# DeltaNet queries, keys and values: 128x128 transposes on TensorE replaced by 32x32 block transposes on VectorE and a trip through DRAM

## The chip, the cores and the metric

The kernel runs on one core of a Trainium2 chip. The metric is the device time of one launch in microseconds (us), lower is better. A core has a matrix engine (TensorE, "PE" in the profile), a vector engine (VectorE, "DVE"), an engine for functions (ScalarE, "ACT"), GpSimd ("POOL") and a queue engine (SyncE, "SP") that issues nearly all transfers of this kernel. SBUF is the on-chip memory of 128 partitions, PSUM the accumulator banks that TensorE writes, DRAM the device memory.

## What is computed

One layer of a hybrid decoder trunk: a normalised input is projected, three groups work on the columns (a gated spatial MLP, eight heads of gated DeltaNet, cross-attention), and one output projection brings them together. The change touches the DeltaNet heads, of 128 columns each:

```python
qkv = causal_conv_silu(jnp.concatenate([d_q, d_k, d_v], axis=-1), conv_w[l])
q, k, v = jnp.split(qkv, 3, axis=-1)
q = l2norm(to_heads(q)) * DN_HEAD_DIM ** -0.5
k = l2norm(to_heads(k))
v = to_heads(v)
...
kb = k * beta[..., None]
a = jnp.where(strict, jnp.einsum('bhnid,bhnjd->bhnij', kb, k) * decay, 0.0)
T = lax.linalg.triangular_solve(a + eye, ...)
attn_intra = jnp.where(tri, jnp.einsum('bhnid,bhnjd->bhnij', q, k) * decay, 0.0)
k_dec = k * jnp.exp(g_last[..., None] - g_cum)[..., None]
...
v_new = val_c - jnp.einsum('bhid,bhde->bhie', kcd_c, state)
o_c = jnp.einsum('bhid,bhde->bhie', qg_c, state) + jnp.einsum('bhij,bhje->bhie', ai_c, v_new)
state = state * jnp.exp(gl_c)[..., None, None] + jnp.einsum('bhid,bhie->bhde', kd_c, v_new)
```

There are 1024 tokens, 2048 model columns, and everything is float32. A norm over a head's 128 columns is needed for every token of q and k.

## The kernel before

**Order of work.** The kernel's body doesn't issue instructions. Each call on `V` (DVE), `S` (ACT), `G` (POOL), `PE` and `Q` (SP) is recorded by `Plan.add` (line 136) with the regions of memory that it reads and writes, and priced by `Plan.price` (line 183): a transpose on PE at its passes, a transfer at its bytes over 350 per ns with 3.8 us of latency, and so on. `Plan.issue` (line 382) lays the operations out several times against these prices, with priorities that come from how late each may be, keeps the layout that ends first, and emits all operations in that order. Each engine then works through its own list strictly in order, and so does SP's queue. The order is fixed when the kernel is built; on the chip only semaphores decide when an instruction may start.

**The matrix work.** The large projections run in stages (`project_stage`, line 1469, over `seven`, line 1290): a 2x2 block scheme in which seven products take the place of eight. Every float32 operand is split in a high and a low part (`split_to`, line 540), and a product is three matmuls (`triple`). The stages that matter here, in order: the projection of heads 0 to 3 (line 1544), that of heads 4 to 7 (line 1559), then the gates `d_z` together with the MLP's `v` (`zv`, line 1657), then the remaining columns, and at the end the output projection, in the order of line 1891.

**The heads.** The tokens are handled in two halves (`hf`) of 512 columns, the heads in pairs. Heads 0 to 3 are called early here, heads 4 to 7 late. For each head and half:

- `conv` (line 947) reads the projected columns, with channels on the partitions and tokens along the row, and makes q, k or v by convolution and SiLU in a tile of 128x512.
- `qk` (line 969) needs k and q with tokens on the partitions: for the sums of squares (`sumsq`, line 965) and for the scaled copy `kd` (`by_token`, line 961). `to_tokens` (line 925) makes them with four PE transposes of 128x128 into one PSUM bank, and ACT reads the bank. Then come the products of k and q with k (the bank again), multiplied by the decays `e` into `gt` and `ai`.
- `front` (line 1182) calls these for two heads, with tiles q, k, kd, ai from `front_sets`: for early heads three sets take turns, for late heads there is one, `own_set`, quarters of the tile `os`. The four tiles are stored to DRAM for later.
- `inverse` (line 1019) inverts diagonal blocks for four pairs and halves at a time on DVE: once for all early heads, once for all late heads.
- `back_of` (line 1565) loads the stored tiles again into one pair of sets (`back_sets`), finishes the inverse (`levels`), makes v (`values`, line 1214: conv, four PE transposes, and `by_token` into the tile `vs`), runs the scan over four steps of 128 tokens and writes the head's output.

In lines 1571 to 1575 the backs of early pairs and the fronts of late pairs alternate. In `heads_out` (line 1159) the output is turned already in the way that the change uses: `turn` (line 936) lets DVE transpose each 32x32 block and stores the tile, `turned_in` (line 941) reads it back with four transfers that put the blocks in their places. The early heads' outputs are read back by `gate` (line 1619), which works on the fresh gate columns in the tiles `obs`, of which there are four.

**Tiles that are shared.** `ring["tn"]` has four tiles, given out in turn. `qk` takes one of them a head for the decay row `vs`, `values` takes one a head for v. Before the backs of late pairs one is taken away (line 1679). `ring["inv"]` gives the split parts in `qk` and the two work tiles of `inverse`. An operation that writes a tile waits for all earlier readers of that part of it.

```python
def to_tokens(*pairs):
    with R.together():
        for src, tp in pairs:
            for tt in range(NT):
                PE.transpose(tp[:, tt * P : (tt + 1) * P], src[:, tt * P : (tt + 1) * P], ident)
    return [tok(tp) for src, tp in pairs]
```

Of the kernel before, what the change touches and what calls it, by code (L numbers as in the profile page):

```python
# [11 lines left out]
AF = mybir.ActivationFunctionType  # L12
# [5 lines left out]
P = 128  # L18
# [4 lines left out]
HT = 512  # L23
# [3 lines left out]
NG, NH, NX = 4, 8, 4  # L27
# [374 lines left out]
def kernel(  # L402
# [29 lines left out]
    V, S, G, PE, Q = R.dve, R.act, R.pool, R.pe, R.sp  # L432
    rank, behind = R.rank, R.behind

    def C(shape, name, dt=F32):
        return sb.tile(list(shape), dt, name=name, tag=name)[:]

    def DT(shape, name, dt=F32):
        return dr.tile(list(shape), dt, name=name, tag=name)[:]
# [41 lines left out]
    def tok(ap):  # L481

        return ap.rearrange("p (t c) -> p t c", c=P)
# [15 lines left out]
    ring = {t: Slots(t, 2, [P, HT]) for t in ("kT", "qT", "vs", "kd", "ai")}  # L499
# [6 lines left out]
    jk = C([P, HT], "jk", mybir.dt.bfloat16)  # L506
# [4 lines left out]
    turn = {"acc": 0, "tp": 0, "dn": 0}  # L511
# [23 lines left out]
    def rsqrt_to(o, a):  # L535
        with rank(1):
            G.tensor_tensor(out=o, in0=a, in1=mhalf[:, : a.shape[1]], op=ALU.pow)


    def split_to(hi, lo, src, eng):  # L540
        S.copy(hi, src)
        eng.tensor_tensor(out=lo, in0=src, in1=hi, op=ALU.subtract)
# [7 lines left out]
    def triple(a, l, r, start, stop, cls=9):  # L550

        mm(a, l[0], r[0], start, False, cls)
        mm(a, l[0], r[1], False, False, cls)
        return mm(a, l[1], r[0], False, stop, cls)
# [181 lines left out]
    for mt in range(2):  # L736
        t = [ring["ai"](F32R) for _ in range(2)]
# [9 lines left out]
    for h in range(NX):  # L747
        t = ring["vs"](F32R).rearrange("p (s m) -> p s m", s=2)
# [60 lines left out]
    def over(bufs):  # L809
        r = Ring("", 0, None)  # L810
        r.bufs = bufs
        return r
# [38 lines left out]
    r3, ww = ([steps[:, i * P : (i + 1) * P] for i in two] for two in ((0, 1), (2, 3)))  # L851
    scs = [C([P, 12, NT, NH], f"sc{hf}") for hf in range(2)]
    gcs, ecs = ([DT([NT, NH, P], f"{n}{hf}") for hf in range(2)] for n in ("gcd", "ecd"))
    e_d = [[DT([P, NT, P], f"ed{hf}_{h}") for h in range(NH)] for hf in range(2)]
    scan_banks, work = dnr.bufs[0:2], over(dnr.bufs[0:2])
    dnab = over(scan_banks)
# [68 lines left out]
# [7 lines that stand above are left out]
    def four(t, order):  # L932

        return t.rearrange(f"p ({order}) -> p t b i", b=4, t=NT)

    def turn(tile, src, dst):

        V.transpose(four(tile, "b t i"), four(src, "t b i"))
        Q.dma_start(dst, tile)

    def turned_in(o, src):

        v = src.rearrange("(a j) (b n) -> b j a n", a=4, b=4)
        for b in range(4):
            Q.dma_start(o[b * 32 : (b + 1) * 32].rearrange("j (a n) -> j a n", a=4), v[b])

    def conv(which, h, hf, o):
        ct = which * NH + h
        xr = ring["xr"]()
        w = [cw[:, k * 24 + ct : k * 24 + ct + 1] for k in range(4)]  # L950
        if hf == 0:
            G.memset(xr[:, 0:3], 0.0)
            Q.dma_start(xr[:, 3:], p_d[which][h][:, 0:HT])
        else:
            Q.dma_start(xr, p_d[which][h][:, HT - 3 :])
        S.activation(o, xr[:, 3:], AF.Copy, scale=w[3])
        for k in range(3):
            V.scalar_tensor_tensor(o, xr[:, k : k + HT], w[k], o, op0=ALU.mult, op1=ALU.add)
        S.activation(o, o, AF.Silu)

    def by_token(o, src, scale):
        for tt in range(NT):
            S.activation(o[:, tt], src[:, tt], AF.Copy, scale=scale[:, tt : tt + 1])

    def sumsq(o, src):
        for tt in range(NT):
            S.activation(jk[:, 0:P], src[:, tt], AF.Square, accum_out=o[:, tt : tt + 1])

    def qk(h, hf, tiles, hs, gt, bank):

        q, k = tiles[:2]
        kd, ai, vs = map(tok, (*tiles[2:4], ring["tn"]()))
        beta, edk = (scs[hf][:, i] for i in (0, 4))
        (kt,) = to_tokens((k, bank))
        sumsq(hs[:, 1], kt)
        V.tensor_scalar(hs[:, 1], hs[:, 1], EPS, None, op0=ALU.add)
        V.reciprocal(hs[:, 3], hs[:, 1])
        V.scalar_tensor_tensor(hs[:, 2], hs[:, 3], -1.0, beta[:, :, h], op0=ALU.mult, op1=ALU.mult)
        V.tensor_tensor(out=hs[:, 3], in0=hs[:, 2], in1=edk[:, :, h], op=ALU.mult)
        by_token(kd, kt, hs[:, 3])  # L980
        e = tok(ring["E"]())
        Q.dma_start(e, e_d[hf][h])
        Q.dma_start(vs, ecs[hf][:, h].partition_broadcast(P))
        by_token(e, e, hs[:, 2])
        (qt,) = to_tokens((q, bank))
        sumsq(hs[:, 0], qt)
        V.tensor_scalar(hs[:, 0], hs[:, 0], P * EPS, P * EPS * EPS, op0=ALU.mult, op1=ALU.add)
        rsqrt_to(hs[:, 4], hs[:, 1])
        V.tensor_tensor(out=hs[:, 4], in0=hs[:, 4], in1=hs[:, 1], op=ALU.mult)

        ch, cl = (ring["inv"](F32R).rearrange("p (t s c) -> p t s c", s=2, c=P) for _ in range(2))
        for i, src in enumerate((k, q)):
            split_to(ch[:, :, i], cl[:, :, i], tok(src), V)
        for t2 in range(NT // 2):
            d = bank
            for j in range(2):
                tt = 2 * t2 + j
                triple(d[:, j * 2 * P : (j + 1) * 2 * P], (ch[:, tt, 0], cl[:, tt, 0]), (ch[:, tt], cl[:, tt]),
                       True, True, R.cls)
            dv = d.rearrange("p (t s c) -> p t s c", s=2, c=P)  # L1000
            ts = slice(2 * t2, 2 * t2 + 2)
            V.tensor_tensor(out=gt[:, ts], in0=dv[:, :, 0], in1=e[:, ts], op=ALU.mult)
            V.tensor_tensor(out=ai[:, ts], in0=dv[:, :, 1], in1=e[:, ts], op=ALU.mult)
        V.tensor_tensor(out=q, in0=q, in1=vs.rearrange("p t c -> p (t c)"), op=ALU.mult)
# [154 lines left out]
    def heads_out(hf, hp, hss, rest):  # L1159
        obs = [vs for kd, ai, vs in rest]  # L1160

        for hs, ob in zip(hss, obs):
            sumsq(hs[:, 5], ob)
            V.scalar_tensor_tensor(hs[:, 6], hs[:, 5], 1.0 / P, hs[:, 0], op0=ALU.mult, op1=ALU.add)
            rsqrt_to(hs[:, 7], hs[:, 6])
            by_token(ob, ob, hs[:, 7])
        for h, (kd, ai, vs) in zip(hp, rest):
            kd, ai, y = (t.rearrange("p t c -> p (t c)") for t in (kd, ai, vs))
            turn(kd, y, o_d[hf][h])
            if h >= NJ:  # L1170
                e = sums()
                Q.dma_start(e, g_d[hf][h - NJ])
                turned_in(ai, o_d[hf][h])
                normed(kd, ai)
                V.tensor_tensor(out=y, in0=kd, in1=e, op=ALU.mult)
                head_done(h, hf, y)
# [5 lines left out]
    def front(p, hf, banks):  # L1182

        hp = (2 * p, 2 * p + 1)
        gt = ring["gt"]().rearrange("p (h t i) -> p h t i", h=2, i=P)
        for i, h in enumerate(hp):
            tiles, hs = front_sets(), ring["hs"]()
            conv(1, h, hf, tiles[1])
            conv(0, h, hf, tiles[0])
            qk(h, hf, tiles, hs, gt[:, i], banks[i])  # L1190
            V.tensor_copy(late_hs[:, hf, h], hs[:, 0:5:4])
            for d, t in zip(late_d[hf][h], tiles[:4]):
                Q.dma_start(d, t)
        gdr = blocks_out(gt, f"{hf}{p}")
        Q.dma_start(gt_d[hf][p].rearrange("p (h t i) -> p h t i", h=2, i=P), gt)
        return gdr
# [16 lines left out]

    def values(hf, hp, gt, qs, ks, hss, rest, inv):
        for i, h in enumerate(hp):
            v = ring["tn"]()
            conv(2, h, hf, v)
            bank = scan_banks[i]
            by_token(rest[i][2], to_tokens((v, bank))[0], hss[i][:, 4])

    def back(hf, hp, gt, qs, ks, hss, rest, inv, ut=None):
        ut = ut or levels(gt, *inv)
# [339 lines left out]
    scan_banks, work = [dnr.bufs[0]] * 2, over(dnr.bufs[0:1])  # L1562
    gdrs = []

    def back_of(p, hf, inv):
        state = front_late(p, hf, inv)
        ut = levels(state[2], *state[-1])
        values(*state)
        back(*state, ut)
# [106 lines left out]
    scan_banks, work = dnr.bufs[0:2], over(dnr.bufs[2:3])  # L1676
# [46 lines left out]
    for n, (tag, to) in enumerate((("gt", mkT), ("inv", mv))):  # L1723
        for i in range(NX // 2):
            t = ring[tag](F32R).rearrange("p (h s m) -> p h s m", h=2, s=2)
# [107 lines left out]
    tn = ring["tn"].bufs  # L1833
# [88 lines left out]
```

## Time and profile before

| | |
|---|---|
| time, median of 3 runs | 1594.69 us (1593.5 to 1596.71) |
| profiled execution: time, span of its instructions | 1593.81 us, 1592.1 us |
| granted TensorE clock, mean | 0.997 |
| instructions | 24568 |
| matmul records on PE (transposes among them) | 8349 |
| bytes moved by transfers | 434.12 MB |

A share is busy time over the span. Busy time of PE counts the union of its records, and since matmuls are pipelined, the record of one (0.39 us for 512 columns) overlaps the next, which starts 0.23 us later; what one occupies is read from the starts. Transposes on PE show as MATMUL with `ident` as one input, block transposes as STREAM_TRANSPOSE on DVE. Nearly all instructions stand under one line, since a plan issues them, so groups are told apart by the names of their tiles: in `out<-in` a name stands without its number, `dn` and `acc` are PSUM banks, `od` is the DRAM tile of the heads' outputs, `sm` the tiles into which `gate` reads it back.

### The profile page before, as it was taken

How to read it: one execution, taken by the hardware profiler on the slowest of the kernel's cores; microseconds unless marked ns; L12 is line 12 of the kernel's file. 1: busy time of each engine (PE TensorE's matmuls, PEld its weight loads, DVE VectorE, ACT ScalarE, POOL GpSimd, SP SyncE). 2: the span in 40 equal slices, each digit the busy share in tenths (PEclk: the TensorE clock that was granted, in tenths of full speed). 3: DMA queues.
4: the chain of work that ended last, by engine and by line, in shares of the span. 5: the costliest groups of instructions: out<-in, count | busy, mean ns of one | idle time of the engine just before them, and what ended most of it. 6: DMA issues, size and time to landing. Idle time of an engine off the chain costs nothing.

```text
span 1592.1 us, 24568 instructions
## 1 busy us (share of the span) xinstructions
PE 1570.2 (99%) x8349; PEld 1315.3 (83%) x8349; DVE 1228.7 (77%) x1818; ACT 963.3 (61%) x2006; POOL 106.7 (7%) x143
## 2 busy tenths in 40 slices
PE   8999999999999999999999989999999999999997
PEld 7988888888887888888888878888888888888886
DVE  6977655877589997777789996867658888688875
ACT  6833255535698436787886557765658864344455
POOL 0100010001000100111111001000000000000001
PEclk9999999999999999999999999999999999999999
DMA  9999966888679898786888988999877989778647
GB/s 320 327 317 346 284 171 183 294 292 245 218 246 315 298 325 254 257 250 205 282 281 277 303 244 245 341 325 309 268 245 253 298 298 347 235 263 293 232 146 276
DMA packets 335951, 434.12 MB, mean 273 GB/s; under 512 B 70089, under 2 KB 160466, under 8 KB 335826
## 3 DMA queue, kind: packets, MB, share of 16 engines
q1 hardware_dynamic: 334098, 429.39, 83.3%
q0 software_dynamic: 1088, 2.10, 0.4%
q8 instruction: 66, 1.08, 0.3%
q10 hardware_dynamic: 640, 1.07, 0.2%
q14 instruction: 59, 0.48, 0.1%
HBM read 332.78 MB, written 99.16 MB: 271 GB/s over the span
## 4 chain that ended last, share of the span: by engine, by line
PE 92%; ACT 3%; DMA 2%; DVE 1%; issue 1%; SPq 0%; POOL 0%; POOLq 0%; ACTq 0%; DVEq 0%
PE acc L398 56%; PE dn L398 35%; ACT jk L398 1%; ACT rhi L398 1%; DMA h0d<-tn 1%; SPq L398 0%; DMA tn<-vd 0%; DMA ut<-in_x_dram 0%; DMA kept<-in_mem_dram 0%; DVE rlo L398 0%; DMA raw<-in_w_in_dram 0%; DVE vs L398 0%; ACT vs L398 0%; DVE tn L398 0%; ACT inv L398 0%
## 5 line engine op out<-in xcount | busy, mean ns | idle before, releaser
L398 PE MATMUL acc<-lh,rhi 128*128 128x512 f32 x1024 | 396.2, 396 | 2.9 <-DVE obs L398 1.2
L398 PE MATMUL acc<-lh,rlo 128*128 128x512 f32 x1024 | 382.9, 397 | 0.0
L398 ACT CAST rhi<-raw 128x1024 fp32r<-128x1024 f32 (+1 forms) x148 | 186.6, 1261 | 248.8 <-PE dn L398 133.8
L398 DVE TENSOR_TENSOR rlo<-raw,rhi 128x1024 fp32r<-128x1024 f32 (+1 forms) x148 | 219.3, 1482 | 109.0 <-ACT rhi L398 98.8
L398 PE MATMUL acc<-ll,rhi 128*128 128x512 f32 x688 | 268.0, 395 | 0.8 <-DVE ll L398 0.8
L398 PEld LDWEIGHTS acc<-lh,rhi 128*128 128x128 f32 x1024 | 192.3, 188 | 41.1 <-issue 1.5
L398 PEld LDWEIGHTS acc<-lh,rlo 128*128 128x128 f32 x1024 | 191.9, 188 | 37.4
L398 DVE TENSOR_TENSOR ll<-ll,lh 128x1024 fp32r<-128x1024 f32 x122 | 148.5, 1217 | 17.3 <-ACT lh L398 17.0
L398 PEld LDWEIGHTS acc<-ll,rhi 128*128 128x128 f32 x688 | 129.6, 189 | 26.4 <-DVE ll L398 1.3
L398 ACT CAST lh<-ll 128x1024 fp32r<-128x1024 f32 x122 | 128.2, 1051 | 29.5 <-PE dn L398 9.0
L398 PE MATMUL acc<-lm,rhi 128*128 128x512 f32 x336 | 130.6, 394 | 0.0
L398 PE MATMUL dn<-lh,rhi 128*128 128x512 f32 x288 | 112.6, 393 | 0.0
L398 PE MATMUL dn<-lh,rlo 128*128 128x512 f32 x288 | 109.7, 393 | 0.0
L398 DVE TENSOR_TENSOR raw<-raw,kept 128x1024 f32<-128x1024 f32 (+1 forms) x56 | 80.9, 1444 | 6.9 <-DMA raw<-in_w_in_dram 5.9
L398 DVE TENSOR_TENSOR rlo<-kept,rhi 128x1024 fp32r<-128x1024 f32 (+1 forms) x29 | 41.8, 1443 | 47.3 <-ACT rhi L398 44.4
L398 PE MATMUL dn<-ll,rhi 128*128 128x512 f32 x192 | 75.2, 393 | 0.0
L398 PEld LDWEIGHTS acc<-lm,rhi 128*128 128x128 f32 x336 | 63.2, 188 | 11.9
L398 ACT CAST rhi<-kept 128x1024 fp32r<-128x1024 f32 (+1 forms) x29 | 35.6, 1229 | 50.3 <-PE dn L398 26.2
L398 PEld LDWEIGHTS dn<-lh,rhi 128*128 128x128 f32 x288 | 54.1, 188 | 10.6
L398 PEld LDWEIGHTS dn<-lh,rlo 128*128 128x128 f32 x288 | 54.0, 188 | 10.5
L398 POOL TENSOR_TENSOR hs<-hs,mhalf 128x4 f32<-128x4 f32 x32 | 48.4, 1515 | 195.3 <-DVE hs L398 194.9
L398 POOL TENSOR_TENSOR small<-small,mhalf 128x1 f32<-128x1 f32 x26 | 21.6, 832 | 562.8 <-DVE small L398 562.8
(421 smaller groups left out, 3449.6 us busy)
## 6 DMA issues: line engine op xcount, KB each, us to landing
raw<-in_w_in_dram SPq DMA_DIRECT2D x120, 512.0 KB
ll<-hsd SPq DMA_DIRECT2D x54, 512.0 KB
raw<-in_w_out_dram SPq DMA_DIRECT2D x48, 512.0 KB
raw<-in_w_in_dram SPq DMA_DIRECT2D x72, 256.0 KB
lm<-hsd SPq DMA_DIRECT2D x26, 512.0 KB
pd<-obs SPq DMA_DIRECT2D x48, 256.0 KB
late<-os SPq DMA_DIRECT2D x44, 256.0 KB
kept<-in_w_in_dram SPq DMA_DIRECT2D x20, 512.0 KB
```

The source lines that it names most:

```text
L398: o.fn(*o.args, **o.kw)
```

## The change

The keys, queries and values take the way of the head outputs. Each of them gets its own DRAM tile (`kt_d`, `qt_d`, `vt_d`), `turn` writes it, `turned_in` reads it. In `qk` k is turned in the tile that becomes `kd`, and read back into the one that becomes `ai`; q is turned in that same tile, once k is done with, and read back into it. In `values` a second `tn` tile holds the turned v, and the read-back goes over v itself. Tokens are then on the partitions, with the 32 columns of a block together but the blocks of one token 128 apart, which the view `four` describes; `like` gives ACT's output the same shape. The PSUM bank is used for the products alone.

```diff
+    kt_d = [[DT([P, HT], f"ktd{hf}_{h}") for h in range(NH)] for hf in range(2)]
+    vt_d = [[DT([P, HT], f"vtd{hf}_{h}") for h in range(NH)] for hf in range(2)]
+    qt_d = [[DT([P, HT], f"qtd{hf}_{h}") for h in range(NH)] for hf in range(2)]
...
     def by_token(o, src, scale):
         for tt in range(NT):
-            S.activation(o[:, tt], src[:, tt], AF.Copy, scale=scale[:, tt : tt + 1])
+            S.activation(like(o[:, tt], src), src[:, tt], AF.Copy, scale=scale[:, tt : tt + 1])
 
     def sumsq(o, src):
         for tt in range(NT):
-            S.activation(jk[:, 0:P], src[:, tt], AF.Square, accum_out=o[:, tt : tt + 1])
+            S.activation(like(jk[:, 0:P], src), src[:, tt], AF.Square, accum_out=o[:, tt : tt + 1])
+
+    def like(o, src):
+
+        return o.rearrange("p (b i) -> p b i", b=4) if len(src.shape) == 4 else o
...
-        (kt,) = to_tokens((k, bank))
+        turn(tiles[2], k, kt_d[hf][h])
+        turned_in(tiles[3], kt_d[hf][h])
+        kt = four(tiles[3], "b t i")
         sumsq(hs[:, 1], kt)
...
-        (qt,) = to_tokens((q, bank))
-        sumsq(hs[:, 0], qt)
+        turn(tiles[3], q, qt_d[hf][h])
+        turned_in(tiles[3], qt_d[hf][h])
+        sumsq(hs[:, 0], four(tiles[3], "b t i"))
...
     def values(hf, hp, gt, qs, ks, hss, rest, inv):
         for i, h in enumerate(hp):
-            v = ring["tn"]()
+            v, t = ring["tn"](), ring["tn"]()
             conv(2, h, hf, v)
-            bank = scan_banks[i]
-            by_token(rest[i][2], to_tokens((v, bank))[0], hss[i][:, 4])
+            turn(t, v, vt_d[hf][h])
+            turned_in(v, vt_d[hf][h])
+            by_token(rest[i][2], four(v, "b t i"), hss[i][:, 4])
```

The two functions that it now calls, as they stood:

```python
def turn(tile, src, dst):
    V.transpose(four(tile, "b t i"), four(src, "t b i"))
    Q.dma_start(dst, tile)

def turned_in(o, src):
    v = src.rearrange("(a j) (b n) -> b j a n", a=4, b=4)
    for b in range(4):
        Q.dma_start(o[b * 32 : (b + 1) * 32].rearrange("j (a n) -> j a n", a=4), v[b])
```

## The prediction

> **What bounds the kernel now.** I read the first part of the page (busy time by engine) and the chain that ended last.
>
> ```profile
> PE 1570.2 (99%) x8349; PEld 1315.3 (83%) x8349; DVE 1228.7 (77%) x1818; ACT 963.3 (61%) x2006; POOL 106.7 (7%) x143
> PE 92%; ACT 3%; DMA 2%; DVE 1%; issue 1%; SPq 0%; POOL 0%; POOLq 0%; ACTq 0%; DVEq 0%
> ```
>
> TensorE (PE) idles 1592.1 - 1570.2 = 21.9 us, and the chain is PE for 92% of the span. So PE work that disappears shortens the run, as long as what replaces it is never late. Next I read stretches of 40 us, to see how much cover there is where the heads are prepared. The columns are PE, weight load, DVE, ACT, POOL, then the granted clock, the DMA share and GB/s.
>
> ```profile
> 120.00:160.00 40.00, 40.00 (x190) 32.89 (x190) 30.75 (x40) 12.71 (x18) 2.19 (x4) 1.00 1.07 346
> 440.00:480.00 40.00, 39.24 (x204) 32.91 (x203) 33.97 (x72) 36.91 (x112) 3.03 (x3) 1.00 0.81 249
> 480.00:520.00 40.00, 39.11 (x202) 31.84 (x202) 36.45 (x65) 35.77 (x110) 3.61 (x5) 1.00 0.95 322
> 520.00:560.00 40.00, 40.00 (x186) 33.27 (x185) 38.82 (x62) 16.24 (x23) 5.63 (x7) 1.00 0.88 293
> 920.00:960.00 40.00, 37.15 (x232) 29.28 (x231) 36.68 (x67) 23.09 (x35) 3.59 (x5) 0.96 0.82 232
> ```
>
> From 440 to 560 VectorE (DVE) is at 109.24 of 120 us. That is the first place where added DVE work has little cover. The DMA share is no wall by itself: in 120 to 160 it is 1.07 at 346 GB/s and PE is still 40.00 of 40.
>
> **Removed: 48 groups of four PE transposes** (8 heads, 2 halves, q, k and v). The timeline of PE around one:
>
> ```profile
> 470.40 0.39 PE L398 MATMUL acc<-ll,rhi 128*128 128x512 f32 x1
> 470.63 0.60 PE L398 MATMUL dn<-ident,kT 128*128 128x128 f32 x4
> 470.99 0.48 PE L398 MATMUL acc<-lh,rlo 128*128 128x512 f32 x1
> 471.30 0.40 PE L398 MATMUL acc<-lh,rhi 128*128 128x512 f32 x1
> 471.54 0.40 PE L398 MATMUL acc<-ll,rhi 128*128 128x512 f32 x1
> ```
>
> Matmuls start 0.23 us apart (470.40 to 470.63). The group starts at 470.63, and the second matmul behind it at 471.30: 0.67 us for the group and one matmul, so the group occupies 0.67 - 0.23 = 0.44 us. 48 x 0.44 = **-21.1 us**. By busy time alone it would be less:
>
> ```profile
> L398 PE MATMUL dn<-ident,os 128*128 128x128 f32 x88 | 13.3, 273 | 0.3 <-ACT os L398 0.3
> L398 PE MATMUL dn<-ident,tn 128*128 128x128 f32 x64 | 9.5, 273 | 0.1
> ```
>
> 22.8 us for 152 of the 192 is 28.8 for all, but this counts the overlapped tails; I take 21.1 from the starts.
>
> **Added on DVE: 48 block transposes** of 128x512. The head outputs already make 16 with the same access pattern:
>
> ```profile
> L398 DVE STREAM_TRANSPOSE kd<-vs 128x512 f32<-128x512 f32 x16 | 11.3, 704 | 4.5 <-ACT vs L398 4.5
> ```
>
> 48 x 0.704 = 33.8 us, DVE goes to 1262.5 us, 79%. Those behind matmul-only stretches cost nothing while DVE has room; in 440 to 560, with 10.8 us free, they push the weight splits back. The Trainium skill ("VectorE: DVE Perf Modes", The three transpose paths, and its rules) speaks against this part: it advises TensorE for 128x128 when the result may lie in PSUM, and gives 390 ns a tile there against 311 ns for DVE's blocks. An estimate by those figures (bf16) would free 192 x 0.39 = 75 us of PE; the starts above show 0.11 us a tile, so here the trace decides, and I do not use it.
>
> **Moved on ACT:** the squares and scalings read SBUF instead of PSUM.
>
> ```profile
> L398 ACT ACTIVATE jk<-dn 128x128 bf16<-128x128 f32 x128 | 36.6, 286 | 6.1 <-PE dn L398 3.8 <-DVE os L398 0.9
> L398 ACT ACTIVATE jk<-vs 128x128 bf16<-128x128 f32 x64 | 20.3, 316 | 0.9
> L398 ACT ACTIVATE vs<-vs,hs 128x128 f32<-128x128 f32 x64 | 21.0, 395 | 0.7 <-POOL hs L398 0.7
> L398 ACT ACTIVATE vs<-dn,hs 128x128 f32<-128x128 f32 x64 | 18.6, 376 | 5.3 <-PE dn L398 5.1
> ```
>
> 128 x (316 - 286) + 128 x (395 - 376) ns = 6.3 us on an engine at 61%: hidden, except in 440 to 520, where ACT has 72.7 of 80.
>
> **Added on the queue:** per transpose one 256 KB store and four 64 KB reads, 240 issues on SP, 25.2 MB.
>
> ```profile
> DMA packets 335951, 434.12 MB, mean 273 GB/s; under 512 B 70089, under 2 KB 160466, under 8 KB 335826
> q1 hardware_dynamic: 334098, 429.39, 83.3%
> ...
> L398 SPq DMA_DIRECT2D od<-kd x16: 319/335/430, 653.7 to 1216.0; - x16
> SPq L398 <- PE dn L398: 203.7, 121, 5.4
> SPq L398 <- DMA od<-kd: 4.0, 4, 2.1
> ```
>
> 5.8% more bytes take the share from 83.3 to about 88%, below what 120 to 160 sustains. SP issues 240 x about 0.43 us = 103 us, while it waits 203.7 us for PE in one row alone. A read-back holds the queue until its store has landed: 4.0 us for 16 round trips now, 12 us for 48, spread out, with the weight loads behind it. I take 0, bounds 0 and 12. For latency, the last head's output shows one whole trip:
>
> ```profile
> 1215.30 0.70 DVE L398 STREAM_TRANSPOSE kd<-vs 128x512 f32<-128x512 f32 x1
> 1216.03 0.32 SPq L398 DMA_DIRECT2D od<-kd  x1
> 1219.07 2.54 SPq L398 DMA_DIRECT2D ai<-od  x4
> 1228.32 0.73 ACT L398 ACTIVATE kd<-ai,col 128x512 f32<-128x512 f32 x1
> ```
>
> 13.0 us from transpose to use, 9.3 of them from the first read; this includes whatever the planned order waits, so it is an upper side. The Trainium skill ("DMA: Bandwidth & Descriptors", Anatomy of one DMA) puts about 2 us of fixed cost on a transfer; an estimate by that is 4 to 5 us a trip. No row here isolates it, and the sum does not use it.
>
> **What the latency delays.** k's read-back and q's transposed tile share the quarter that ends as `ai`, so within a head they follow each other: read k 9.3, four squares with their accumulator reads about 2.0, the small operations and the scaling 2.1, q's trip 13.0, squares 2.0, the two products 0.8, the store of `ai` until the quarter is free again about 5.6: **35 us a head** in one set of tiles. The late heads have one set (`own_set`). The issue rows of the pairs' block stores and of the early heads' last outputs show today's pace:
>
> ```profile
> 749.00 1.84 SPq L398 DMA_DIRECT2D gdr<-gt  x4
> ...
> 814.88 2.53 SPq L398 DMA_DIRECT2D gdr<-gt  x4
> ...
> 837.27 0.43 SPq L398 DMA_DIRECT2D od<-kd  x1
> ...
> 843.40 1.75 SPq L398 DMA_DIRECT2D sm<-od  x4
> ```
>
> A pair takes 66 us there, 70 will do. But `values` now takes two of the four `tn` tiles a head, so a pair takes all four, and its second head uses those in which the previous late pair keeps its decay rows until its last product. The early backs are thereby tied to the late fronts. Their last values and the last gate:
>
> ```profile
> 778.07 1.14 ACT L398 ACTIVATE vs<-dn,hs 128x128 f32<-128x128 f32 x4
> 855.77 0.68 DVE L398 TENSOR_TENSOR obs<-obs,sm 128x512 f32<-128x512 f32 x1
> 867.53 0.68 DVE L398 TENSOR_TENSOR obs<-acc,yz 128x512 f32<-128x512 f32 x1
> ```
>
> The gate at 855.77 frees the output tile that the next eviction needs at 867.53: 11.8 us of slack, so values by 778 + 12 = 790. The late fronts can finish their first head about 585 to 590, once the inverse of the early ones (DVE busy to about 565) has moved some 10 to 15 us; the third pair is done five heads later, 585 + 175 = 760 to 765; conv and trip of v add about 20: 780 to 785. That just fits. The late pairs' own backs end later too, which the last rival prices.
>
> **Sum.** -21.1 (PE) + 4 (DVE and ACT full in 440 to 560: with 16 early transposes, 11.3 us, against 10.8 free, part of them movable ahead; bounds 0 and 11) + 4 (queue hops on the tied chain; bounds 0 and the rivals) = -13 us. The profiled execution took 1593.81, 1.7 beyond its span; it lies 0.9 below the median 1594.69. From the median: **1582 us**.
>
> **Rivals.** *All hidden (0.08):* 1594.7 - 21.1 = 1573.6. For: 120 to 160 shows PE full under the heaviest DMA. Against: DVE at 38.82 of 40 in 520 to 560.
> *Washed out (0.08):* the 21 us return as small waits, within 0.2% (3 us, about what a measurement tells from no change).
> *Slower, the early gates come late (0.27):* with 45 us a head instead of 35 (ten hops through engines that are full) the third late pair ends 585 + 225 = 810, values 830, 40 us past 790; PE stops at the output tiles: 1594.7 - 21.1 + 39 = 1613. It decides from about 41 us a head (585 + 205 + 20 = 810, 20 past 790). Against: the planner may start the late fronts earlier.
> *Slower, the late heads come late (0.15):* before their backs `tn` loses one of its tiles, so with two per value the second head's turn waits for the first's scaling, some 18 us in each of four backs, 72 us. Outputs end at 1216 + 72 = 1288, and the late inverse may come 30 us later, 1318; sums follow in about 20. The chain shows where PE needs them:
>
> ```profile
> 1320.56 23.19 PE dn L398 x102
> 1343.76 65.28 PE acc L398 x288
> ```
>
> The run from 1343.76 is the first that uses sums of both halves. At 1338 that fits by 6 us; with 30 us more it costs 24 to 30: 1594.7 - 21.1 + 30 = 1604.
> *It does not do what it says:* excluded by the diff, the 192 transposes have no other caller left.
>
> **Numbers.** Forecast 0.42. Faster = 0.42 + 0.08 = 0.50; same 0.08; slower 0.27 + 0.15 = 0.42. The forecast's own range is 1574 to 1590. To hold 8 in 10 it reaches from 1571 to 1617, past the first slow rival's price.
>
> **What would show it.** PE with 192 fewer matmuls and about 21 us less work; `STREAM_TRANSPOSE` x72 instead of 24 near 0.70 us; DMA near 459 MB. The forecast fails if PE idles much over 30 us: before outputs named `obs` around 840 to 900 for the first slow rival, behind tiles of sums near 1320 to 1345 for the second, behind `rlo` or `ll` in 440 to 600 if DVE decides. A trip shorter than 13.0 us, or late pairs closing faster than every 70 us, would put it towards 1574.

## The result and the profile after

The changed kernel takes 1709.28 us (median of 4 runs, 1707.23 to 1710.59), the kernel before 1594.1 (4 runs, 1593.49 to 1596.71): a ratio of 1.0718, 95% interval [1.0699, 1.0737], 115 us slower. The forecast was 1582 us and the range ended at 1617: wrong in sign, and outside the range.

The page of the changed kernel: busy time by engine, transfers, and the chain that ended last.

```profile
span 1706.9 us, 24653 instructions
...
PE 1585.2 (93%) x8157; PEld 1315.8 (77%) x8157; DVE 1267.9 (74%) x1866; ACT 980.9 (57%) x2004; POOL 95.3 (6%) x143
...
DMA packets 370513, 459.30 MB, mean 269 GB/s; under 512 B 73929, under 2 KB 188882, under 8 KB 370386
...
PE 75%; DMA 6%; DVE 5%; ACT 3%; issue 2%; SPq 2%; POOL 0%; POOLq 0%; DVEq 0%; ACTq 0%
```

PE has the 192 matmuls fewer (8349 - 8157), but its busy time rose by 15.0 us and its idle time from 21.9 to 1706.9 - 1585.2 = 121.7 us. Together 114.8, the whole difference of the spans. The stretches show where (columns as before: PE, weight load, DVE, ACT, POOL, granted clock, DMA share, GB/s; first some of 40 us, then three longer ones):

```profile
560.00:600.00 40.00, 25.06 (x94) 19.46 (x94) 25.69 (x41) 20.19 (x50) 4.50 (x7) 0.81 0.92 290
...
880.00:920.00 40.00, 23.29 (x83) 18.41 (x84) 24.84 (x41) 22.42 (x56) 0.00 (x0) 0.64 0.69 221
920.00:960.00 40.00, 23.51 (x131) 19.99 (x129) 22.27 (x50) 24.40 (x84) 3.51 (x7) 0.79 0.89 281
...
440.00:640.00 200.00, 165.60 (x707) 133.75 (x706) 156.82 (x269) 114.56 (x273) 10.41 (x17) 0.91 0.86 279
...
800.00:1080.00 280.00, 210.79 (x1009) 170.43 (x1008) 205.93 (x370) 160.00 (x375) 18.37 (x25) 0.85 0.80 242
1080.00:1710.00 630.00, 616.18 (x3281) 513.92 (x3279) 482.88 (x662) 376.65 (x717) 22.44 (x32) 0.99 0.84 277
```

PE idles 200 - 165.60 = 34.4 us in 440 to 640 and 69.2 us in 800 to 1080; from 1080 to the end of the span, 627 us, only 10.7. Where it has gaps, the other engines have too: from 560 DVE has 25.69 of 40 us, ACT 20.19. No engine is full in the stretches of 40 us, and the DMA share is below the 1.07 at which PE ran without a gap before. Everybody waits for a chain. The waits of PE over the whole run don't name one culprit:

```profile
PE dn L398 <- DVE os L398: 23.5, 2, 19.6
PE acc L398 <- ACT rhi L398: 20.9, 7, 4.9
PE dn L398 <- DVE obs L398: 13.1, 2, 8.7
```

The block transposes stand as foreseen, 72 of them in six groups at 703 to 709 ns. The two largest new groups (by form, busy us and mean ns):

```profile
L398 DVE STREAM_TRANSPOSE os<-os 128x512 f32<-128x512 f32 x22 | 15.5, 706 | 5.6 <-ACT os L398 3.9 <-DMA late<-os 1.7
L398 DVE STREAM_TRANSPOSE tn<-tn 128x512 f32<-128x512 f32 x16 | 11.3, 705 | 0.7 <-ACT vs L398 0.2 <-ACT tn L398 0.2
```

So the chain must be followed by its tiles. First the queue's timeline around the first late head (head 4): `ktd` and `qtd` are the DRAM tiles of k and q, `od` that of the heads' outputs; the columns are start and length of the issue, a transfer lands later.

```profile
584.95 1.08 SPq L398 DMA_DIRECT2D os<-ktd  x2
...
700.72 0.34 SPq L398 DMA_DIRECT2D od<-kd  x1
702.29 0.32 SPq L398 DMA_DIRECT2D od<-kd  x1
703.46 0.41 SPq L398 DMA_DIRECT2D qtd<-os  x1
...
740.48 0.33 SPq L398 DMA_DIRECT2D qtd<-os  x1
...
786.98 0.34 SPq L398 DMA_DIRECT2D od<-kd  x1
789.63 0.34 SPq L398 DMA_DIRECT2D qtd<-os  x1
791.63 0.51 SPq L398 DMA_DIRECT2D od<-kd  x1
829.11 0.32 SPq L398 DMA_DIRECT2D qtd<-os  x1
...
877.79 1.78 SPq L398 DMA_DIRECT2D od<-kd  x2
...
953.66 1.80 SPq L398 DMA_DIRECT2D od<-kd  x2
```

Then ACT's timeline of the same kernel, its squares alone (out of `vs`: a head's outputs; out of `os`: head 4's k):

```profile
696.01 0.31 ACT L398 ACTIVATE jk<-vs 128x128 bf16<-128x128 f32 x1
696.83 0.31 ACT L398 ACTIVATE jk<-os 128x128 bf16<-128x128 f32 x1
```

The last read of head 4's k was issued by 586.03 (584.95 + 1.08), and ACT, which is busy 57% of the span, takes its first square at 696.83, 111 us later: right behind the last square of the first back's outputs. From there backs and late fronts go in lockstep: two outputs (700.72, 702.29), two q (703.46, 740.48), two outputs (786.98, 791.63), two q (789.63, 829.11), and so on. Nothing in the data asks for that. All `sumsq` calls, k's, q's and the outputs', write their squares, which nobody reads, to the same 128 columns of the scratch tile `jk` (only `accum_out` is used). `Plan.add` takes a write after a write for a dependence, so all sums of squares of all heads are put in the order of the program, and there backs and late fronts alternate. Since all are ACT's own instructions, no semaphore shows it: the order is written into ACT's list.

The order isn't new. In the kernel before, PE transposes head 4's k at 545.19, and ACT takes its first square 104 us later, again right behind the last square of the first back's outputs (first line PE, the others ACT):

```profile
545.19 0.60 PE L398 MATMUL dn<-ident,os 128*128 128x128 f32 x4
...
649.20 0.31 ACT L398 ACTIVATE jk<-vs 128x128 bf16<-128x128 f32 x1
649.69 0.28 ACT L398 ACTIVATE jk<-dn 128x128 bf16<-128x128 f32 x1
```

What is new is the length of the links. The outputs of the four early pairs and halves leave there at

```profile
653.73 1.08 SPq L398 DMA_DIRECT2D od<-kd  x2
...
709.32 0.34 SPq L398 DMA_DIRECT2D od<-kd  x1
...
760.96 0.42 SPq L398 DMA_DIRECT2D od<-kd  x1
...
828.68 0.32 SPq L398 DMA_DIRECT2D od<-kd  x1
```

In the changed kernel the first leaves 700.72 - 653.73 = 47.0 us later, and a round, one back and one late front, takes (953.66 - 700.72) / 3 = 84.3 us instead of (828.68 - 653.73) / 3 = 58.3. So the fourth is 47 + 3 x 26 = 125 us late, and the run loses 115.

### The profile page after: what moved, and what is told of

It reads as the page before. It is cut to its first block, busy times and chain, and to the rows that moved or that the text cites. A ratio compares the mean times of both kernels' runs of the same rounds, so it can differ in the third digit from the quotient of the medians.

```text
span 1706.9 us, 24653 instructions
## 1 busy us (share of the span) xinstructions
PE 1585.2 (93%) x8157; PEld 1315.8 (77%) x8157; DVE 1267.9 (74%) x1866; ACT 980.9 (57%) x2004; POOL 95.3 (6%) x143
## 2 busy tenths in 40 slices
DMA packets 370513, 459.30 MB, mean 269 GB/s; under 512 B 73929, under 2 KB 188882, under 8 KB 370386
## 3 DMA queue, kind: packets, MB, share of 16 engines
q10 hardware_dynamic: 640, 1.07, 0.2%
## 4 chain that ended last, share of the span: by engine, by line
PE 75%; DMA 6%; DVE 5%; ACT 3%; issue 2%; SPq 2%; POOL 0%; POOLq 0%; DVEq 0%; ACTq 0%
PE acc L398 46%; PE dn L398 29%; SPq L398 2%; DMA ll<-hsd 1%; DVE os L398 1%; DMA mixd<-obs 1%; DVE inv L398 1%; ACT rhi L398 1%; DVE raw L398 1%; DVE rlo L398 1%; ACT jk L398 0%; DMA lm<-h0d 0%; DMA kept<-in_w_in_dram 0%; DMA raw<-in_w_in_dram 0%; ACT vs L398 0%
## 5 line engine op out<-in xcount | busy, mean ns | idle before, releaser
L398 PE MATMUL acc<-lh,rlo 128*128 128x512 f32 x1024 | 378.0, 398 | 4.0 <-DVE rlo L398 4.0
L398 PEld LDWEIGHTS acc<-lh,rhi 128*128 128x128 f32 x1024 | 195.9, 193 | 72.9 <-ACT rhi L398 23.0
L398 DVE TENSOR_TENSOR ll<-ll,lh 128x1024 fp32r<-128x1024 f32 x122 | 148.5, 1217 | 21.9 <-ACT lh L398 21.7
L398 PE MATMUL dn<-lh,rhi 128*128 128x512 f32 x288 | 115.4, 403 | 13.1 <-DVE obs L398 13.1
L398 DVE TENSOR_TENSOR lm<-lm,lh 128x1024 fp32r<-128x1024 f32 x42 | 52.1, 1240 | 9.9 <-ACT lh L398 9.9
L398 ACT CAST lh<-lm 128x1024 fp32r<-128x1024 f32 x42 | 44.0, 1048 | 23.9 <-DMA lm<-h0d 6.6
```

What stands on the lines that cost most here:

```text
L398: o.fn(*o.args, **o.kw)
```

## The experiments

**One operand at a time, and two.** The changed kernel with only k, only q, only v the new way, and with k and q. For what stays on PE the old lines are put back:

```diff
-        turn(tiles[3], q, qt_d[hf][h])
-        turned_in(tiles[3], qt_d[hf][h])
-        sumsq(hs[:, 0], four(tiles[3], "b t i"))
+        (qt,) = to_tokens((q, bank))
+        sumsq(hs[:, 0], qt)
```

> Only the keys take the new way; queries and values are transposed on TensorE as before. Load theory (the extra 16 VectorE transposes, 8.4 MB and 80 issues slow the kernel in proportion): a third of the 115 us, about 1632 us. Scratch theory (all sums of squares write the same 128 columns of the scratch tile jk and are recorded in program order; what is slow is a trip that starts after a head's squares of k and must end before its squares of q): k's trip can start before any squares, so no trip lies in that chain, 1585 to 1600 us. Shared-quarter theory (k's read-back and q's trip follow each other in the quarter that becomes ai): one trip alone costs little, 1585 to 1605 us.

> Only the queries take the new way. Load theory: about 1632 us. Scratch theory: q's tile no longer waits for anything of k, so its trip starts ahead of the squares, 1585 to 1600 us. Shared-quarter theory: the quarter holds q alone, 1585 to 1605 us.

> Only the values take the new way (one more of the four tn tiles per value). Load theory: about 1632 us. Scratch theory: no squares of v, so nothing by itself, but its tiles tie backs to fronts: 1590 to 1615 us. Shared-quarter theory says nothing of v; the tile theory of the prediction says that the early gates come late, 1600 to 1630 us.

> Keys and queries take the new way, values not. Load theory: two thirds, about 1670 us, the sum of the two single runs. Scratch theory and shared-quarter theory: far more than the sum of the two single runs, 1665 to 1695 us, with the early heads' queries going out one head after another some 22 us apart, as in the changed kernel.

Ratios to the kernel before: keys 1.0011 [1.0001, 1.002], queries 1.005 [1.0029, 1.0071], values 1.015 [1.0134, 1.0165], keys and queries 1.0555 [1.0538, 1.0573]. Keys and queries together cost 88 us, where each alone costs 2 and 8: a cost of transposes, bytes or issues would add up, a chain needn't. Queries and values alone lie 2 and 3 us above the ranges that the scratch theory gave them. With one trip a head, the trip can run ahead of the squares. With both, q is turned in the tile that k's read-back occupies until k's scaling, which follows k's squares: the whole trip of q then lies between two places of the one order of squares. The shared quarter alone would foretell this jump too; the four slices below part the two theories. Keys alone also show what a third of the removed PE work is worth, from the page of that kernel:

```profile
PE 1564.5 (98%) x8285; PEld 1309.1 (82%) x8285; DVE 1238.1 (78%) x1834; ACT 967.4 (61%) x2005; POOL 96.1 (6%) x143
```

PE is busy 5.7 us less than before (1570.2), where a third of 21.1 would be 7.0, and its idle time (span 1589.9) is 25.4 instead of 21.9. Even there, little of the gain reaches the time.

**The scratch tile.** The changed kernel with four slices of `jk` in turn, and the same edit on the kernel before as a control:

```diff
+    squares = over([jk[:, i * P : (i + 1) * P] for i in range(4)])
+
     def sumsq(o, src):
+        scratch = squares()
         for tt in range(NT):
-            S.activation(like(jk[:, 0:P], src), src[:, tt], AF.Square, accum_out=o[:, tt : tt + 1])
+            S.activation(like(scratch, src), src[:, tt], AF.Square, accum_out=o[:, tt : tt + 1])
```

> The changed kernel with every transpose, byte and issue kept; only the sums of squares write their squares (which nobody reads) to four slices of the scratch tile in turn instead of one. Load theory: no change, 1700 to 1715 us. Shared-quarter theory: no change either. Scratch theory: the heads' chains come apart, most of the 115 us goes, 1610 to 1650 us, and the early queries go out closer together than 22 us.

> The control: the kernel before with the same four slices. Scratch theory: without a trip between the squares the order costs nothing, 1588 to 1600 us. If it were faster by much, the slices would be worth something by themselves and the run above would say less.

With slices 1649.55 us, ratio 1.0337 [1.0312, 1.0362]: 60 of the 115 us are gone with the same transposes, bytes and issues. The control is at 1.0029 [1.0018, 1.004]: the kernel before loses nothing by the one slice, although it binds there too. With slices head 4's k is squared 99 us earlier than at 649.69, and nothing is gained:

```profile
550.22 0.28 ACT L398 ACTIVATE jk<-dn 128x128 bf16<-128x128 f32 x1 [1.22 <-PE dn L398]
```

`Plan.issue` lays out each variant anew, so a run shows what is lost without one tie, not exactly what the tie costs in the changed kernel's own layout.

**The sum of q apart.** A second order that the data don't ask for: regions are recorded in blocks of 32 elements, so q's squares, whose sums go to `hs[:, 0]`, wait for the scaling of `e`, which reads `hs[:, 2]` in the same block, and so for a free `E` tile.

```diff
-        sumsq(hs[:, 0], four(tiles[3], "b t i"))
-        V.tensor_scalar(hs[:, 0], hs[:, 0], P * EPS, P * EPS * EPS, op0=ALU.mult, op1=ALU.add)
+        sumsq(hs[:, 8], four(tiles[3], "b t i"))
+        V.tensor_scalar(hs[:, 0], hs[:, 8], P * EPS, P * EPS * EPS, op0=ALU.mult, op1=ALU.add)
```

> The changed kernel, the sum of q's squares written to another column of the small tile hs (its ninth), outside the 32-element region in which the planner tracks the columns before: q's squares then need not wait for the scaling of the decays e, which waits for one of two tiles. Scratch theory: the chain over the heads stays, so only a part goes, 1675 to 1700 us. Load theory: 1700 to 1715 us.

1688.11 us, 1.0586 [1.0559, 1.0614]: 21 us back. The inverse of the early heads starts at 583.0 there, 25 us before the changed kernel's 608.2. It was not tried together with the slices, so the two gains can't be added.

**Which squares.** The changed kernel in which only the outputs' squares have a slice of their own; those of k and q still share one.

```diff
-    def sumsq(o, src):
+    def sumsq(o, src, at=0):
...
-            S.activation(like(jk[:, 0:P], src), src[:, tt], AF.Square, accum_out=o[:, tt : tt + 1])
+            S.activation(like(jk[:, at : at + P], src), src[:, tt], AF.Square, accum_out=o[:, tt : tt + 1])
...
-            sumsq(hs[:, 5], ob)
+            sumsq(hs[:, 5], ob, P)
```

> The changed kernel, in which only the squares of the heads' outputs get a slice of the scratch tile of their own; k's and q's squares still share one. If the 60 us of the four slices come from the alternation of backs and late fronts, this run falls from 1709 to 1650 to 1670 and the late fronts' first store of q moves from 703 to about 635 us. If they come from the order among the fronts, it stays at 1690 to 1710.

1654.32 us, 1.0365 [1.0342, 1.0387]: this one address gives back 55 of the 60 us. The queue's timeline of this kernel:

```profile
585.10 1.77 SPq L398 DMA_DIRECT2D os<-ktd  x4
...
611.35 0.35 SPq L398 DMA_DIRECT2D qtd<-os  x1
615.58 1.81 SPq L398 DMA_DIRECT2D os<-qtd  x4
...
699.17 0.32 SPq L398 DMA_DIRECT2D qtd<-os  x1
...
719.98 0.37 SPq L398 DMA_DIRECT2D od<-kd  x1
...
771.27 0.40 SPq L398 DMA_DIRECT2D od<-kd  x1
...
830.75 0.43 SPq L398 DMA_DIRECT2D od<-kd  x1
...
899.28 0.34 SPq L398 DMA_DIRECT2D od<-kd  x1
...
928.89 0.34 SPq L398 DMA_DIRECT2D qtd<-os  x1
```

and three instructions of head 4: the first square of its k on ACT, the transpose of its q on DVE, and the first square of its q:

```profile
597.47 0.31 ACT L398 ACTIVATE jk<-os 128x128 bf16<-128x128 f32 x1
...
607.84 0.71 DVE L398 STREAM_TRANSPOSE os<-os 128x512 f32<-128x512 f32 x1
...
621.13 0.31 ACT L398 ACTIVATE jk<-os 128x128 bf16<-128x128 f32 x1 [0.41 <-DMA os<-qtd]
```

The reads of head 4's k are issued at the same time as in the changed kernel (585.10 to 586.87), and it is squared 10.6 us later instead of 111; its q leaves at 611.35 instead of 703.46, earlier than expected (635). The lockstep is gone: a round of outputs takes (899.28 - 719.98) / 3 = 59.8 us, nearly the 58.3 of the kernel before, and the last q leaves at 928.89, where the alternating kernel had its last at 995.49. The early fronts gained nothing, as the start of the inverse on DVE shows (first and last of its squarings; the changed kernel, then this one, then the one with four slices; before, 540.5 to 938.4):

```profile
L398 DVE TENSOR_TENSOR sq<-inv,inv x62: 180/357/426, 608.2 to 1079.5; 128x31 f32<-128x31 f32 x4, 128x60 f32<-128x60 f32 x4, 128x87 f32<-128x87 f32 x4, 128x112 f32<-128x112 f32 x4
```

```profile
L398 DVE TENSOR_TENSOR sq<-inv,inv x62: 179/357/425, 613.1 to 1014.8; 128x31 f32<-128x31 f32 x4, 128x60 f32<-128x60 f32 x4, 128x87 f32<-128x87 f32 x4, 128x112 f32<-128x112 f32 x4
```

```profile
L398 DVE TENSOR_TENSOR sq<-inv,inv x62: 175/356/425, 542.1 to 978.1; 128x31 f32<-128x31 f32 x4, 128x60 f32<-128x60 f32 x4, 128x87 f32<-128x87 f32 x4, 128x112 f32<-128x112 f32 x4
```

The early inverse is as late as in the changed kernel (613.1 against 608.2), and the late one starts its last squaring 65 us earlier. So the order between backs and late fronts is what lengthened the rounds. The 60 us that this run still loses lie, as far as its rows go, in its start: the first outputs leave at 719.98, 66 us after the 653.73 of the kernel before. Four slices take the order among the early fronts away as well; the inverse starts at 542.1 again and the first outputs leave at 634.6, and yet the run is only 5 us faster. It loses its time elsewhere, PE is busy 150.89 of the 200 us in 440 to 640 where it has 176.84 with the outputs apart. What the order among the early fronts costs by itself can't be read from these two runs.

**What is left with four slices: 54 us by the ratio.** Four slices, with parts on PE again: keys and queries of heads 0 to 3 alone, of heads 4 to 7 alone, of all heads; values alone. The edit of the first two:

```diff
-        turn(tiles[2], k, kt_d[hf][h])
-        turned_in(tiles[3], kt_d[hf][h])
-        kt = four(tiles[3], "b t i")
+        if h < NJ:
+            turn(tiles[2], k, kt_d[hf][h])
+            turned_in(tiles[3], kt_d[hf][h])
+            kt = four(tiles[3], "b t i")
+        else:
+            (kt,) = to_tokens((k, bank))
```

and q likewise (`h >= NJ` in the second).

> Four slices as above; only heads 0 to 3 take keys and queries the new way, heads 4 to 7 (one set of tiles) and all values as before. Scratch theory: early heads have three sets, so nothing is left of the loss, 1580 to 1600 us. Shared-quarter theory: still a loss, 1610 us or more. Load theory: a third of the loss, about 1632 us.

> Four slices, keys and queries of heads 4 to 7 alone the new way, values as before. If the late heads' one set of tiles is what costs, this run takes all that the run with keys and queries of all heads takes over the kernel before (20 us or more). If the late heads have room and only early and late together exceed it (the late fronts begin later because the early ones end later), it stays within 8 us of the kernel before, at 1594 to 1602.

> Four slices of scratch, keys and queries of all heads the new way, values by TensorE as before. The kernel with four slices and all three the new way took 1649.55 us, 56 more than the kernel before; keys and queries of the early heads alone took 1595.98. If the rest sits in the values (two tn tiles for each, which tie early backs to late fronts), this run falls to 1600 or below. If it sits in the late heads, whose one set of tiles must hold k's and q's trips one behind the other, it stays at 1615 to 1645. If each gives half, about 1620.

> Four slices, values alone the new way, with two tn tiles for each value. Values alone with one slice took 1618.12, 24 more than the kernel before. If that came through the order of the squares (a value's trip delays a back, and the squares of its outputs stand ahead of the next front's), this run falls to 1594 to 1600. If it came through the tn tiles, it stays at 1612 to 1620.

Early keys and queries 1.002 [1.0006, 1.0033], late ones 1.0094 [1.0078, 1.0109], both 1.0183 [1.0163, 1.0203], values 1.0037 [1.0025, 1.0049]. In us at 1594: 3, 15, 29 and 6. The parts don't add up here either: 18 against 29 for early and late, and 29 + 6 = 35 against 54 (0.0337 x 1594) for all three operands. The early heads, which have three sets of tiles, hide two trips; the late ones, which have one, don't. The late heads' 15 us lie between the two theories (20 or more, 8 or less). In their run the block stores of the late pairs start (901.35 - 671.80) / 3 = 76.5 us apart, in the kernel before (859.67 - 693.68) / 3 = 55.3: two trips in one set are the likely reason, but no run gave the late heads a second set. Where early and late together lose their 11 us more can be read, why cannot: in 440 to 640 PE idles 37.9 us with both and 10.1 with the late ones alone.

**The tn tiles.** v turned in `vs`, which takes the scaled v afterwards, so that a value needs one `tn` tile as in the kernel before; once for values alone with one slice, once for all three with four:

```diff
-            v, t = ring["tn"](), ring["tn"]()
+            v, t = ring["tn"](), rest[i][2].rearrange("p t c -> p (t c)")
```

> One slice of scratch as in the kernel before, values alone the new way, but v is turned in the tile vs that takes the scaled v afterwards: one tn tile for each value, as in the kernel before. If the 24 us of values alone came through the tn tiles, this run falls to 1594 to 1600; if through the order of the squares or the trip's length alone, it stays at 1612 to 1620. Should both this run and the one with four slices fall, the loss needs both bindings at once.

> Four slices, keys, queries and values the new way, v turned in the tile vs: one tn tile for each value instead of two. The kernel with four slices and two tn tiles took 1649.55, that without the values 1623.45. If the values' 26 us come through the tn tiles, this run falls to 1623 to 1632; if not (the trips lengthen the backs, which alternate with the fronts on the same engines and queue), it stays at 1642 to 1656.

Alone 1.0123 [1.0106, 1.0141] against 1.015 with two tiles: a few us of 24 at most. With four slices 1.0324 [1.0301, 1.0347] against 1.0337: nothing that can be told. The tie is there, for with values alone the late pairs' block stores start 68.4 us apart with two tiles and 60.2 with one, but little of it reaches the time. The `tn` tiles are not where the values cost. Values alone lost 24 us with one slice and 6 with four: most of theirs, too, went through the order of squares. Why they cost 25 us (54 - 29) on top of keys and queries when that order is gone stays open.

**The last output and the end.** The last store of an output (`od`, the end of the range in its row) in the changed kernel:

```profile
L398 SPq DMA_DIRECT2D od<-kd x16: 319/341/547, 700.7 to 1331.8; - x16
```

With the outputs apart it comes at 1278.4, with four slices at 1275.1, with keys and queries and four slices at 1244.0, with the late ones alone at 1228.5. From it to the end of the span it is 375.1, 374.9, 374.5, 378.7 and 379.0 us in these five kernels (spans 1706.9, 1653.3, 1649.6, 1622.7, 1607.5), and in the kernel before 1592.1 - 1216.0 = 376.1. Of the ten kernels not shown here seven lie between 370 and 380 us and three (early keys and queries, values, and one `tn` tile with four slices) between 383 and 388. What the last output loses, the run loses, nearly one for one. This doesn't say that PE waits for the last output: in the changed kernel it idles 10.7 us in all from 1080 on. PE has lost the time before, in the stretches above, and the outputs and the end are late together.

## Why the prediction was wrong

**The step that failed** is in the part on latency: "The late fronts can finish their first head about 585 to 590", and with it "That just fits". The late fronts don't run free of the early backs. One order of squares ties them, and in the kernel before it already holds head 4's k, the first late one, back to 649.69, in the trace that the prediction had. With 650 for 585 its own working would have given 650 + 175 + 20 = 845 for the last early values, 55 us past the 790 that it allowed. The change then lengthened this chain at two places: the first outputs leave 47 us later, and each of the three rounds behind them takes 26 us longer. The prediction named the `tn` tiles as what couples early backs and late fronts; the two runs with one `tn` tile show that this tie costs next to nothing. It never asked which tiles the *moved* operations write: the squares were costed (6.3 us on ACT) and not placed.

**A second step failed:** the inverse of the early heads was to move 10 to 15 us and moved 67.7 (540.5 to 608.2). The early heads have three sets of tiles, and the prediction took this for room; in the changed kernel their squares follow one another in program order, and with four slices the inverse is back at 542.1. The 47 us at the first outputs stand behind this. The run with the outputs apart, in which the inverse stays late, keeps 60 us of the loss.

**A third:** the last rival put its loss near 1320 to 1345, where PE needs the sums, and priced 72 us of lateness at 24 to 30. The last output is 115.8 us later (1331.8 - 1216.0), but PE loses its time long before, in 440 to 640 and 800 to 1080, and next to nothing from 1080 on. The slack of 6 us was not put to the test. The direction of that rival, late heads late, was right; its cause, its place and its price weren't.

**The pace of the late heads** was mis-sized on the side of the kernel before. "A pair takes 66 us there, 70 will do" reads the longest of three distances: the pairs' block stores there start at 693.68, 749.00, 814.88 and 859.67, on average 55.3 us apart. The 35 us a head were near: without the lockstep the late heads' q leave, from the second one on, (928.89 - 699.17) / 6 = 38.3 us apart. The first two are 87.8 us apart (611.35 to 699.17); what holds the second is not shown. q's trip took 13.3 us from its transpose (607.84) to its first square (621.13), just above the 13.0 that were taken as an upper side. The late heads' keys and queries by themselves cost 15 us, where the sum had 4 for the tied chain.

**Right:** 192 matmuls, 72 transposes at 0.70 us, 459.30 MB, no full DVE (25.69 of 40 us from 560, where PE has gaps), and the first sign of failure, PE idle beyond 30 us. The sign of the first slow rival, waits before `obs`, is there with 13.1 us in all, of which 4.4 (before 904.23) lie near the place foretold, and explains little. The 21.1 us of removed PE work are real but not seen whole: 5.7 of the 7.0 for keys alone. (The 28.8 us by busy time are more than these 21.1, not less, as the prediction has it; it did not use them.) In the changed kernel PE's busy time rises instead; the last section shows what the clock has to do with it.

**Open:** what the order among the early fronts costs by itself, the 25 us of the values on top of keys and queries, and why early and late keys and queries cost 11 us (29 - 18) more together than apart. Giving the late heads a second set of tiles was not tried. No variant was faster than the kernel before.

## What to carry to other kernels

When a step gets a longer latency, list everything that it *writes*, dummy outputs too: a scratch tile whose contents nobody reads is a dependence for whoever orders the program, and it is harmless only as long as all its writers come quickly one after another. Before that, look up in the trace of the old kernel where the operations to be moved stand: the first late square stood there 64 us behind the time from which the prediction counted. Price a longer step not by its busy time but by the number of times that it lies on a chain, and look for the chain in the rows where all engines are half idle. Test a suspected order by giving its parts different memory: here one changed address gave back 55 of 115 us.

## What the hardware showed beyond that

PE's busy time depends on its idle time. The changed kernel and the one with four slices issue the same 8157 matmuls; PE is busy 1585.2 us in the first and 1569.2 in the second, from its page:

```profile
PE 1569.2 (95%) x8157; PEld 1307.2 (79%) x8157; DVE 1266.7 (77%) x1866; ACT 980.8 (59%) x2008; POOL 101.1 (6%) x143
```

The granted clock is 0.962 in the first and 0.979 in the second, and the stretches above show it at 0.64 to 0.81 where PE has 23 to 25 of 40 us, and at 0.99 from 1080 on, where PE is nearly full. PE's timeline in the changed kernel, behind a wait of 4.38 us, shows the single matmuls:

```profile
904.23 0.80 PE L398 MATMUL dn<-lh,rhi 128*128 128x512 f32 x1 [4.38 <-DVE obs L398]
904.82 0.63 PE L398 MATMUL dn<-lm,rhi 128*128 128x512 f32 x1
905.24 0.63 PE L398 MATMUL dn<-lh,rlo 128*128 128x512 f32 x1
...
909.36 0.40 PE L398 MATMUL dn<-lh,rhi 128*128 128x512 f32 x1
909.59 0.40 PE L398 MATMUL dn<-lm,rhi 128*128 128x512 f32 x1
```

They start 0.42 us apart up to 909.08, the ten starts from 904.82 in 4.26 us, and 0.23 us apart from 909.36 on. At 0.23 us the ten would take 2.3 us, so this wait cost about 2 us on top of its length (an estimate from these rows). In the whole run it is up to 16 us; how much of the 16 is the clock was not parted from other effects of gaps on the count of busy time. The Trainium skill ("TensorE: Matmul & The Clock Gate", Part 1) says that the clock is halved after about 3.4 us of idleness and comes back after about as much work; the trace agrees in kind, nearly twice the distance for 4.9 us (904.23 to 909.08) behind 4.38 us of waiting, while the threshold itself is not measured here.
